# Meta rows of an output projection computed from one 34-column stationary operand

## The chip, the cores and the metric

The kernel is one program on one core of a Trainium2 chip. A core has TensorE (PE in the profile; PEld is its loading of stationary operands), VectorE (DVE), ScalarE (ACT), GpSimd (POOL) and a queue SP that issues the DMA transfers. Each engine takes its own instructions in a fixed order and waits at the first that is not ready. The metric is the device time of one execution in microseconds (us), lower is better.

## The reference

One layer of a hybrid decoder on 1024 tokens of width 1024, with 16 learned meta tokens put in front:

```python
h = concat([meta, x])                       # 1040 rows
a = rmsnorm(h, ln_mix_pre)
dq, dk, dv, hq, hf, hi, hg = split(a @ w_in)
mix = concat([diff_attention(dq, dk, dv), hgrn2(hq, hf, hi, hg)]) @ w_out
h = h + rmsnorm(mix, ln_mix_post)
a = rmsnorm(h, ln_ffn_pre)
u = causal_conv(a @ w_up, width 3)          # token t sees t-2, t-1, t
h = h + rmsnorm((gelu(gate) * up) @ w_down, ln_ffn_post)
return h[16:]
```

The meta rows are dropped at the end. After the mixing step only the last two of them still matter, because the width-3 convolution of the first real token looks back at two rows. So the output projection `@ w_out` is computed for 1024 token rows and two meta rows.

## The kernel before, in words

All large products are made in split precision: an operand is kept as a rounded part (`hi`) and a remainder (`lo`), and a product is three matmuls, hi·hi, hi·lo and lo·hi. A split of a weight tile is a copy on ACT (the rounded part) and a subtraction on POOL or DVE (the remainder); `split` is that helper. Recorded through a helper, every DVE, ACT and POOL instruction has line L54, so tiles, and not lines, tell them apart.

The stretch that matters lies between the last input projections and the feed-forward network:

- **First half of the output projection** (`out_first`): output columns 0 to 511, token blocks 1 to 8 in order, for the seven 128-row slices k = 0 to 6 of the mixed features. Each block is 21 matmuls of 512 columns (lines L972, L974, L976 in `out_part`; tile `py`, stationary operand `mp`). Behind block 4 come the two meta rows (stationary `m`, two columns wide): 7 slices × 3 matmuls. Slice k = 7 is not there yet: it is the last head of the HGRN recurrence, `hgrn_head`, which is interleaved with these matmuls by `interleave`, by a count of estimated PE time. That head has a pass over seven levels (tile `pl`, lines L417 and L423); between two levels DVE multiplies `kr` and `hq`, and the next level's matmuls read the result. Then follow the state chain (`pk`, `kn`, `pu`, `st`, `po`) and the normalised outputs (`on`, `ss`).
- Meanwhile the weights of the second half (`wor1`, split into `woh` and `wol`, `load_wo`) and those of the feed-forward network (`ra`, split into `uh` and `ul`, `prep_plain` and `prep`) are loaded and split. A raw tile can be overwritten by a later load only when its split is done, so SP waits for POOL or DVE there.
- **Second half**: columns 512 to 1023, the same blocks, all eight slices. Block 1 is followed by the meta rows (tile `py1_0`, 8 slices × 3 matmuls), then `out_last` for some blocks, which adds slice 7 to the first half (tile `pz`). `post(i)` normalises a block on ACT and DVE, adds the residual and normalises again; `trans(i)` transposes the result on PE (L1174, tile `pa`) two blocks later, `post(0)`'s during block 4.

PE's order is the order written in the program. The orders on DVE, ACT, POOL and SP in this part are chosen by a scheduler from the dependencies and its own estimates, except where `issue_after` ties an instruction to another.

Of the kernel before, what the change touches and what calls it, by code (L numbers as in the profile page):

```python
# [9 lines left out]
F32 = mybir.dt.float32  # L10
F32R = mybir.dt.float32r
U8 = mybir.dt.uint8
AF = mybir.ActivationFunctionType
ALU = mybir.AluOpType
# [3 lines left out]
P = 128  # L18
META = 16
SEQ = 1024  # L20
L = META + SEQ
D = 1024
KD = D // P
# [63 lines left out]
def layer_kernel(ctx: ExitStack, tc: tile.TileContext, x, meta, table, lbl, gpre, gpost, win,  # L87
# [3 lines left out]
    V, A = Ordered(tc, nc.vector, state), Ordered(tc, nc.scalar, state)  # L91
    G = Ordered(tc, nc.gpsimd, state)
    T, SY = nc.tensor, nc.sync
# [19 lines left out]
    def const(shape, name, dt=F32):  # L113
        return cp.tile(shape, dt, tag=name, name=name)
# [12 lines left out]
    nlam = const([P, 1], "nlam")  # L127
    cwt = const([P, 2 * NF, 3], "cwt")
    cbt = const([P, 2 * NF], "cbt")
    m0 = const([P, 2, KD, 2], "m0", F32R)  # L130

    hsc = dp.tile([SEQ, D], F32, tag="hsc", name="hsc")
    gsc = dp.tile([DFF, SEQ], F32, tag="gsc", name="gsc")
# [390 lines left out]
    def normed(k, b0, src, on, ss, C, n, gain, nm, raw=None, gate=None):  # L524
        if gate is None:
            V.scalar_tensor_tensor(ss[:C, :n], ss[:C, :n], 1.0 / 128, ss[:C, 4:4 + n], ALU.mult, ALU.add)
            A.activation(ss[:C, :n], ss[:C, :n], AF.Ln)
            A.activation(ss[:C, :n], ss[:C, :n], AF.Exp, scale=-0.5)
        else:
            rstd_of(ss[:C, :n], ss[:C, :n], 128.0)  # L530
        V.tensor_tensor(on[:C, :n], src, ss[:C, :n].rearrange("p (n o) -> p n o", o=1).to_broadcast([C, n, P]), op=ALU.mult)
        yield 1
        pt = ps_m(f"ss{nm}")
        W = start(b0 + n - 1) + rows(b0 + n - 1) - start(b0)
        for c in range(n):
            o = max(W - (n - c) * C, 0)
            T.transpose(pt[:, o:o + C], on[:C, c], ident[:C, :C])
        if gate is None:
            raw = on.rearrange("p n c -> p (n c)")[:, :W]
            A.mul(raw, pt[:, :W], gain)  # L540
        else:
            V.scalar_tensor_tensor(raw, pt[:, :W], gain, gate, ALU.mult, ALU.mult)

        def halves(hi, lo, cols):
            A.copy(hi, raw[:, cols])
            V.tensor_tensor(lo, raw[:, cols], hi.bitcast(F32), op=ALU.subtract)

        if b0 == 0:
            halves(m0[:, 0, k], m0[:, 1, k], slice(META - 2, META))
        first = max(b0, 1)  # L550
        if b0 + n > first:
            w = P * (b0 + n - first)
            m = parts_tile(nm)
            halves(m[:, 0, :w], m[:, 1, :w], slice(W - w, W))
            parts_store(k, first, b0 + n, m, 0)
        yield 1
# [410 lines left out]
    def out_part(m, py, wo, ks, first, last):  # L967
        r = m.shape[-1]
        for k in ks:
            hi, lo = wo[k]  # L970
            mh, ml = m[:, 0, k], m[:, 1, k]
            T.matmul(py[:r], mh, hi, start=(first and k == ks[0]), stop=False)  # L972
            yield 216
            T.matmul(py[:r], mh, lo, start=False, stop=False)  # L974
            yield 216
            T.matmul(py[:r], ml, hi, start=False, stop=(last and k == ks[-1]))  # L976
            yield 216

    SLOTS = (("X1", "X2", "mp", "X1", "X2", "mp", "X1", "X2"), ("mp", "X1", "X2", "mp", "X1", "X2", "X1", "mp"))

    def block_tile(n, i):
# [30 lines left out]
    def out_last(p):  # L1012
        r = tok(p)[0]
        py = ps_b(f"pz{p}")
        m = m0[:, :, KD - 1:] if p == 0 else k7(p)
        for _ in out_part(m, py, wo0[KD - 1:], range(1), True, True):
            pass
        V.tensor_tensor(y0[:r, p], y0[:r, p], py[:r], op=ALU.add)
        junk = qp.tile([P, 512], F32, tag="junk", name=f"jz{p}", bufs=1)
        A.activation(junk[:r], y0[:r, p], AF.Square, accum_out=ssy[:r, p, 0:1])  # L1020
        A.activation(ssy[:r, p, 0:1], ssy[:r, p, 0:1], AF.Identity, bias=eps[:r], scale=1.0 / D)
        if p < 3:
            y0_gain(p)

    def out_first():
        pys = {}
        steps = [(1, 0), (2, 0), (1, 1), (2, 1), (1, 2), (2, 2)] + [(i, c) for i in range(3, NBLK) for c in range(3)]
        KS = (range(0, 2), range(2, 4), range(4, 7))
        for i, c in steps:
            if c == 0:  # L1030
                pys[i] = ps_s(f"py0_{i}")[:, 0] if i < 3 else ps_in(f"py0_{i}")
                if 2 < i + 1 < NBLK:
                    first_load(i + 1)
                elif i == NBLK - 1:
                    second_load(1)
            yield from out_part(blocks[i], pys[i], wo0, KS[c], c == 0, c == 2)
            if c == 2:
                A.copy(y0[:, i], pys.pop(i))
            if i == 4 and c == 2:
                py = ps_in("py0_0")  # L1040
                yield from out_part(m0, py, wo0, range(7), True, True)
                A.copy(y0[:2, 0], py[:2])

    interleave(out_first(), [hgrn_head(t_h, set())] + carried(), FO, 4200)
    close(h_cm, at_p_cm, p_cm)
# [81 lines left out]
    def load_xh(i):  # L1127
        r = tok(i)[0]
        if i:
            xhs[i] = qp.tile([P, D], F32, tag="xh", name=f"xh{i}")  # L1130
        else:
            xhs[i] = ep.tile([P, D], F32, tag="e0", name="xh0")
        SY.dma_start(xhs[i][:r], meta[14:16, :] if i == 0 else x[P * (i - 1): P * i, :])

    def post(i, py):
        r, t0 = tok(i)
        xh = xhs.pop(i)
        if i % 2:
            a2 = long_tile(f"a2_{i}")[:, :D]
        elif i == 0:  # L1140
            a2 = xh
        else:
            a2 = bp.tile([P, D], F32, tag="a2", name=f"a2_{i}", bufs=1)
        tmp = qp.tile([P, 512], F32, tag="tmp", name=f"tmp{i}", bufs=1)
        junk = qp.tile([P, 512], F32, tag="junk", name=f"junk{i}", bufs=1)
        s1, s2 = ssy[:r, i, 1:2], ssy[:r, i, 2:3]
        A.activation(junk[:r], py[:r], AF.Square, accum_out=s1)
        V.tensor_tensor(tmp[:r], py[:r], gpo[:r], op=ALU.mult)
        A.activation(s1, s1, AF.Ln, bias=ssy[:r, i, 0:1], scale=1.0 / D)
        A.activation(s1, s1, AF.Exp, scale=-0.5)  # L1150
        V.scalar_tensor_tensor(xh[:r, :512], y0[:r, i], s1, xh[:r, :512], ALU.mult, ALU.add)
        V.scalar_tensor_tensor(xh[:r, 512:], tmp[:r], s1, xh[:r, 512:], ALU.mult, ALU.add)
        if i:
            SY.dma_start(hsc[P * (i - 1): P * i, :], xh)
        if i:
            A.activation(a2[:r], xh[:r], AF.Square, accum_out=s2)
        else:
            s3 = ssy[:r, i, 3:4]
            for half, s_ in ((0, s2), (1, s3)):
                A.activation(py[:r], xh[:r, 512 * half:512 * half + 512], AF.Square, accum_out=s_)  # L1160
            V.tensor_tensor(s2, s2, s3, op=ALU.add)
        rstd_of(s2, s2, D)
        V.scalar_tensor_tensor(a2[:r], xh[:r], s2, gfb[:r], ALU.mult, ALU.mult)
        a2t[i] = a2
# [49 lines left out]
    def run(*args):  # L1214
        for _ in out_part(*args):
            pass

    def k7(i):
        return m7[:, i - 1:i].rearrange("p b l t -> p l b t")

    for i in range(1, NBLK):
        py = ps_b(f"py1_{i}")
        if i >= 3:
            y0_gain(i)
        if i == 1:
            load_xh(1)
            load_xh(0)
        if i + 1 < NBLK:
            second_load(i + 1)
            load_xh(i + 1)  # L1230
        run(blocks[i], py, wo, range(4), True, False)
        if i == 3:
            trans(1)
        if i == 4:
            trans(0)
        if i > 3:
            trans(i - 2)
        run(blocks[i], py, wo, range(4, 7 if i == 1 else 8), False, i > 1)
        if i == 1:
            pm = ps_b("py1_0")  # L1240
            run(m0, pm, wo, range(KD), True, True)
            for p in range(3):
                out_last(p)
            run(k7(1), py, wo[KD - 1:], range(1), False, True)
            post(1, py)
            post(0, pm)
            for p in (3, 4):
                out_last(p)
            continue
        post(i, py)  # L1250
        if i == 5:
            t_split(0, 0, quarter(0, 0), ep, "e0")
            t_split(0, 4, quarter(0, 4), ep, "e1")
        if i == 7:
            t_split(0, 7, quarter(0, 7), mxp, "X2", WN[0])
            t_split(0, 6, quarter(0, 6), mxp, "X1", WN[0])
        if i in (2, 3):
            for p in (1 + 2 * i, 2 + 2 * i):
                out_last(p)
# [382 lines left out]
```

## Time and profile before

| what | value |
|---|---|
| median of 3 runs | 1322.26 us (1322.09 to 1323.52) |
| profiled execution: its time | 1325.6 us |
| profiled execution: its span | 1323.8 us |
| mean granted TensorE clock | 0.997 |
| PE busy | 1286.8 us, 97% of the span |
| DVE / ACT / POOL busy | 930.1 / 692.5 / 455.4 us |

A row of the timeline gives the start, the duration, the engine, the line, the operation, output and inputs, the shapes, and in brackets the engine's idle time just before it and what ended that. Matmuls overlap, so the start-to-start distance, not the duration, is what one costs. A row of the waits gives the total, the number and the longest wait. A row of the windows gives busy time and number of instructions of each engine in a stretch, then the granted TensorE clock, the share of DMA busy time and the GB/s.

### The profile page before, as it was taken

To read this page: it belongs to the slowest core of one execution; us is meant where nothing else is said; L and a number is where in the kernel's file an instruction comes from. 1 tells how busy PE (TensorE), PEld (TensorE's weight loads), DVE (VectorE), ACT (ScalarE), POOL (GpSimd) and SP (SyncE) were. 2 spreads that over 40 slices of the span, in tenths; PEclk is the share of its full clock that TensorE was granted. 3 is DMA by queue.
4 is the path that set the end of the run, shared out by engine and by line. 5 is a ranking of instruction groups with operands and counts; after the bars stand their busy time and mean duration, and the time that the engine had idled before them with its cause. 6 is when DMAs were issued, how large, how long until landed. Compare 5 with 4: busy or idle time off the path is not lost.

```text
span 1323.8 us, 26191 instructions
## 1 busy us (share of the span) xinstructions
PE 1286.8 (97%) x10172; PEld 1185.5 (90%) x10172; DVE 930.1 (70%) x1531; ACT 692.5 (52%) x1635; POOL 455.4 (34%) x340
## 2 busy tenths in 40 slices
PE   8999999999999999899999999999999999999997
PEld 7899999899999988677999999999999997888875
DVE  6464646465645564547997788989989967697586
ACT  8475466547544754246754444444444435454553
POOL 5211211121112111243077667676676730010121
PEclk9999999999999999999999999999999999999999
DMA  5111121112111335487232234545445428865363
GB/s 209 61 40 33 54 57 41 49 46 65 44 42 41 88 101 169 153 277 254 81 112 80 80 95 154 177 144 173 154 144 166 144 84 275 312 205 166 88 206 120
DMA packets 99427, 165.00 MB, mean 125 GB/s; under 512 B 10035, under 2 KB 34899, under 8 KB 99302
## 3 DMA queue, kind: packets, MB, share of 16 engines
q1 hardware_dynamic: 99302, 163.32, 37.8%
q8 instruction: 80, 1.31, 0.4%
q14 instruction: 45, 0.37, 0.1%
HBM read 122.65 MB, written 40.63 MB: 123 GB/s over the span
## 4 chain that ended last, share of the span: by engine, by line
PE 45%; DVE 11%; ACT 3%; issue 3%; DMA 2%; POOL 0%; SPq 0%; DVEq 0%; ACTq 0%; POOLq 0%
PE pd L1491 5%; PE pd L1492 5%; PE pd L1490 5%; DVE c L54 5%; PE pb L1316 4%; PE pb L1317 3%; PE pb L1318 3%; PE pa L1316 2%; PE pa L1317 2%; PE pa L1318 2%; PE pc L1316 2%; PE pc L1317 2%; PE pc L1318 2%; PE py L976 1%; PE py L972 1%
## 5 line engine op out<-in xcount | busy, mean ns | idle before, releaser
L1316 PE MATMUL pb<-t,uh 128*128 128x258 f32 x504 | 144.0, 286 | 8.9 <-DVE u L54 8.9
L1318 PE MATMUL pb<-t,ul 128*128 128x258 f32 x504 | 141.6, 281 | 0.0
L1317 PE MATMUL pb<-t,uh 128*128 128x258 f32 x504 | 141.6, 281 | 0.0
L1491 PE MATMUL pd<-wl,gh 128*128 128x512 f32 x308 | 122.0, 396 | 1.2 <-DVE wl L54 1.1
L1492 PE MATMUL pd<-wh,gl 128*128 128x512 f32 x308 | 121.7, 395 | 0.0
L1490 PE MATMUL pd<-wh,gh 128*128 128x512 f32 x308 | 121.7, 395 | 0.0
L54 POOL TENSOR_TENSOR c<-c,c 128x514 f32<-128x514 f32 (+1 forms) x44 | 75.2, 1709 | 121.1 <-ACT c L54 111.4
L1316 PEld LDWEIGHTS pb<-t,uh 128*128 128x128 f32 x504 | 95.4, 189 | 12.2 <-DVE u L54 12.1
L54 DVE SCALAR_TENSOR_TENSOR c<-uu,cwt,c 128x514 f32<-128x514 f32 (+1 forms) x88 | 89.2, 1023 | 19.3 <-ACT c L54 19.0
L1317 PEld LDWEIGHTS pb<-t,uh 128*128 128x128 f32 x504 | 95.6, 190 | 0.0
L1318 PEld LDWEIGHTS pb<-t,ul 128*128 128x128 f32 x504 | 95.2, 189 | 0.0
L1316 PE MATMUL pa<-t,uh 128*128 128x258 f32 (+1 forms) x336 | 95.2, 283 | 0.0
L1318 PE MATMUL pa<-t,ul 128*128 128x258 f32 (+1 forms) x336 | 95.0, 283 | 0.0
L1317 PE MATMUL pa<-t,uh 128*128 128x258 f32 (+1 forms) x336 | 94.8, 282 | 0.0
L1316 PE MATMUL pc<-t,uh 128*128 128x258 f32 (+1 forms) x336 | 94.4, 281 | 0.0
L1317 PE MATMUL pc<-t,uh 128*128 128x258 f32 (+1 forms) x336 | 94.0, 280 | 0.0
L1318 PE MATMUL pc<-t,ul 128*128 128x258 f32 (+1 forms) x336 | 93.7, 279 | 0.0
L54 DVE SCALAR_TENSOR_TENSOR c<-ug,cwt,c 128x514 f32<-128x514 f32 (+1 forms) x88 | 89.6, 1019 | 0.9 <-ACT c L54 0.6
L54 ACT CAST uh<-ra 128x512 fp32r<-128x512 f32 x67 | 41.0, 616 | 66.4 <-PE pb L1317 48.2
L1491 PEld LDWEIGHTS pd<-wl,gh 128*128 128x128 f32 x308 | 57.7, 187 | 16.5 <-DVE wl L54 2.7
L54 POOL TENSOR_TENSOR ul<-ws,uh 128x512 fp32r<-128x512 f32 x42 | 64.7, 1541 | 20.4 <-ACT uh L54 20.4
L1492 PEld LDWEIGHTS pd<-wh,gl 128*128 128x128 f32 x308 | 57.7, 187 | 14.4 <-DVE gl L54 0.4
(373 smaller groups left out, 4161.2 us busy)
## 6 DMA issues: line engine op xcount, KB each, us to landing
ra<-in_wup_dram SPq DMA_DIRECT2D x88, 256.0 KB, 3.0
mp<-msc SPq DMA_DIRECT2D x23, 512.0 KB, 6.0
wd<-in_wdown_dram SPq DMA_DIRECT2D x44, 256.0 KB, 3.3
tsc<-wd SPq DMA_DIRECT2D x44, 256.0 KB, 3.2
wi<-tsc SPq DMA_DIRECT2D x44, 256.0 KB, 2.9
gi<-gsc SPq DMA_DIRECT2D x33, 256.0 KB, 4.1
wi<-in_wdown_dram SPq DMA_DIRECT2D x33, 256.0 KB, 5.3
gsc<-c SPq DMA_DIRECT2D x22, 257.0 KB, 2.3
```

The costliest lines, as they stand in the source:

```text
L54: ins = call(*args, **kw)
L972: T.matmul(py[:r], mh, hi, start=(first and k == ks[0]), stop=False)
L976: T.matmul(py[:r], ml, hi, start=False, stop=(last and k == ks[-1]))
L1316: T.matmul(pt, hi[:, s], th[:, k], start=(first and k == 0), stop=False, skip_group_check=True)
L1317: T.matmul(pt, hi[:, s], tl[:, k], start=False, stop=False, skip_group_check=True)
L1318: T.matmul(pt, lo[:, s], th[:, k], start=False, stop=(k == 3), skip_group_check=True)
L1490: T.matmul(py, gh[:, s], wh, start=(k == 0 and pr not in (3, 7)), stop=False, skip_group_check=True)
L1491: T.matmul(py, gh[:, s], wl, start=False, stop=False, skip_group_check=True)
L1492: T.matmul(py, gl[:, s], wh, start=False, stop=(k == NH - 1), skip_group_check=True)
```

## The change

The two meta rows of slices 0 to 6 were kept as a tile `m0[part, slice, 2]`; now they lie in one row of 46 columns, the rounded parts at columns 2k and the remainders at 32 + 2k, the rest set to zero. Slice 7 has its own tile `m0_7`. A stationary operand of 34 columns from column 2k then holds both parts of slice k, at output rows 0 to 1 and 32 to 33 (the rows between are not used), so one matmul with `hi` gives hi·hi and lo·hi, and a second with `lo` and two columns gives hi·lo. The two pairs of rows are brought together by ACT copies and an addition on GpSimd, once in each half. In the second half slice 7 is done right behind slice 0, with three matmuls as before. `post(0)` reads the sum from SBUF and not from PSUM, and stands behind `post(2)`, no longer behind `post(1)`.

```diff
-    m0 = const([P, 2, KD, 2], "m0", F32R)
+    m0 = const([P, 46], "m0", F32R)
+    G.memset(m0.bitcast(F32), 0.0)
+    m0_7 = const([P, 2, 1, 2], "m0_7", F32R)
...
-            halves(m0[:, 0, k], m0[:, 1, k], slice(META - 2, META))
+            hl = [m0_7[:, l, 0] if k == KD - 1 else m0[:, 32 * l + 2 * k:32 * l + 2 * k + 2] for l in range(2)]
+            halves(hl[0], hl[1], slice(META - 2, META))
...
+    def meta_part(py, wo, full):
+        for k in range(KD - 1):
+            hi, lo = wo[k]
+            both = [(34, hi), (2, lo)]
+            if k == KD - 2:
+                both.reverse()
+            for i, (r, w) in enumerate(both):
+                T.matmul(py[:r], m0[:, 2 * k:2 * k + r], w, start=(k == 0 and i == 0), stop=(r == 34 and k == KD - 2))
+                yield 216
+            if k == 0 and full:
+                yield from out_part(m0_7, py, wo[KD - 1:], range(1), False, False)
...
-        m = m0[:, :, KD - 1:] if p == 0 else k7(p)
+        m = m0_7 if p == 0 else k7(p)
...
-                yield from out_part(m0, py, wo0, range(7), True, True)
+                yield from meta_part(py, wo0, False)
+                part = ap_.tile([P, L], F32, tag="q0", name="part")[:2, :512]
                 A.copy(y0[:2, 0], py[:2])
+                A.copy(part, py[32:34])
+                G.tensor_tensor(y0[:2, 0], y0[:2, 0], part, op=ALU.add)
...
-            xhs[i] = ep.tile([P, D], F32, tag="e0", name="xh0")
+            both = ep.tile([P, 2 * D], F32, tag="e0", name="xh0")
+            xhs[i], xhs["sum"] = both[:, :D], both[:, D:]
...
-    def post(i, py):
+    def post(i, py, free=None):
...
-                A.activation(py[:r], xh[:r, 512 * half:512 * half + 512], AF.Square, accum_out=s_)
+                A.activation(free[:r], xh[:r, 512 * half:512 * half + 512], AF.Square, accum_out=s_)
...
-            run(m0, pm, wo, range(KD), True, True)
+            for _ in meta_part(pm, wo, True):
+                pass
             for p in range(3):
                 out_last(p)
             run(k7(1), py, wo[KD - 1:], range(1), False, True)
             post(1, py)
-            post(0, pm)
+            ysum = xhs.pop("sum")
+            for l in range(2):
+                A.copy(ysum[:2, 512 * l:512 * l + 512], pm[32 * l:32 * l + 2])
+            G.tensor_tensor(ysum[:2, :512], ysum[:2, :512], ysum[:2, 512:], op=ALU.add)
             for p in (3, 4):
                 out_last(p)
             continue
         post(i, py)
+        if i == 2:
+            post(0, ysum[:, :512], ysum[:, 512:])
```

The scheduler's orders move with it. In the built program, on POOL the subtractions of `wor1` slices 0 and 2 stand ahead of the four `ul` subtractions of `prep_plain`, which had been ahead of them; the new addition of the meta rows stands between. On SP the four `ra` loads of `prep_plain`, the load of the meta residual and the first `ra` load of `prep` stood ahead of block 3's load and now stand around block 8's, so their ACT copies `uh` fall into the recurrence's state chain. On DVE the subtraction `wol` of `wor1` slice 3 stood between the products of levels 5 and 6 and now stands between those of levels 3 and 4; that of slice 1 moves up by one level, into the place of a `ul`, and that `ul` moves into the state chain.

## The prediction

> **What bounds the kernel now.** First the page: PE is busy almost throughout, so what PE does not issue, or does not wait for, is time, unless a wait takes its place.
>
> ```profile
> span 1323.8 us, 26191 instructions
> PE 1286.8 (97%) x10172; PEld 1185.5 (90%) x10172; DVE 930.1 (70%) x1531; ACT 692.5 (52%) x1635; POOL 455.4 (34%) x340
> ```
>
> Then the windows around the projection: PE's one lean and slow place is 530 to 550, and 540 to 550 is the only ten microseconds in which the granted clock falls while work goes on.
>
> ```profile
> 530.00:540.00 10.00, 8.51 (x188) 5.61 (x188) 7.22 (x8) 0.00 (x0) 8.10 (x6) 1.00 0.61 194
> 540.00:550.00 10.00, 7.43 (x39) 4.39 (x37) 4.62 (x8) 3.18 (x7) 0.00 (x0) 0.83 0.58 203
> ```
>
> Then the timeline of PE there: levels 5, 6 and 7 of the last recurrence head (`pl`), and the meta matmuls (`m`) between them.
>
> ```profile
> 533.65 0.40 PE L972 MATMUL py<-woh,mp 128*128 128x512 f32 x1
> 534.15 0.73 PE L423 MATMUL pl<-hq,kr 128*32 128x16 f32 x64
> 538.80 0.70 PE L417 MATMUL pl<-hq,kr 128*32 128x32 f32 x32 [1.16 <-DVE hq L54]
> 539.42 0.39 PE L972 MATMUL py<-woh,m 128*2 128x512 f32 x1
> 544.70 1.72 PE L417 MATMUL pl<-hq,kr 128*64 128x64 f32 x16 [2.57 <-DVE hq L54]
> 546.35 0.58 PE L976 MATMUL py<-woh,m 128*2 128x512 f32 x1
> 548.01 0.57 PE L972 MATMUL py<-woh,mp 128*128 128x512 f32 x1
> 548.89 0.39 PE L972 MATMUL py<-woh,mp 128*128 128x512 f32 x1
> ```
>
> Last the chain of waits, which says what held DVE back: three `ul` subtractions and a `wol` on POOL, behind them a load, its ACT copy, DVE, and only then PE.
>
> ```profile
> 530.01 5.12 POOL ul L54 x3
> 535.13 1.27 POOL wol L54
> 536.42 5.57 DMA wor<-in_wout_dram
> 542.01 0.63 ACT woh L54
> 543.27 0.69 DVE kr L54
> 543.95 0.61 DVE hq L54
> 544.70 1.72 PE pl L417 x16
> ```
>
> In DVE's timeline `wol` of `wor1` slice 3 blocks the queue for 3.81 us, and before that a product beside POOL's `ul` takes 1.79 us where it takes 0.69 without:
>
> ```profile
> 528.20 0.69 DVE L54 TENSOR_TENSOR hq<-hq,t 128x520 f32<-128x520 f32 x1
> 532.21 1.79 DVE L54 TENSOR_TENSOR hq<-hq,tt 128x520 f32<-128x520 f32 x1
> 542.66 0.69 DVE L54 TENSOR_TENSOR wol<-wor,woh 128x512 fp32r<-128x512 f32 x1 [3.81 <-ACT woh L54]
> ```
>
> **Removed matmuls.** 7 + 7 matmuls go. The 24 meta matmuls of the second half, first and last:
>
> ```profile
> 580.36 0.39 PE L972 MATMUL py<-woh,m 128*2 128x512 f32 x1
> 585.67 0.40 PE L976 MATMUL py<-woh,m 128*2 128x512 f32 x1
> L972 PEld LDWEIGHTS py<-woh,mp x119: 186/188/329, 510.2 to 638.9; 128*128 128x128 f32 x119
> ```
>
> They are 5.31/23 = 0.231 us apart, and a 34-column load cannot cost more than the 128-column one, 0.188 us, which hides under that. So 14 × 0.231 = 3.2 us, 1.6 in each half; in the first half only if PE does not then wait for DVE.
>
> **The moved subtractions, first half.** PE's work and order up to level 4 are the same. POOL's `ul` no longer stand in front: `wol` of slices 0 and 2 start when the recurrence's products end.
>
> ```profile
> 528.30 6.83 POOL L54 TENSOR_TENSOR ul<-ra,uh 128x512 fp32r<-128x512 f32 x4
> 535.10 3.00 POOL L54 TENSOR_TENSOR wol<-wor,woh 128x512 fp32r<-128x512 f32 x2
> ```
>
> The first, at 3.00/2 = 1.5 us, ends at 529.8, and SP may issue `wor1` slice 3. Its landing took 5.57 us before, behind a 900 KB load. Now nothing is issued ahead of it for six microseconds. The eight landings around here, of `wor` and then of `ra`, were:
>
> ```profile
> DMA to landing us min/median/max: 3.6/4.2/5.6
> DMA to landing us min/median/max: 2.6/3.9/9.2
> ```
>
> I take 3.6, the fastest `wor`, since its queue is the emptiest; bounds 2.6 and 5.57. From landing to PE the chain above took 544.70 − 541.99 = 2.71 us (ACT copy, `wol`, `kr`, `hq`). But `wol` now blocks the products of level 4, so it is level 5 that waits: 529.8 + 3.6 + 2.7 = 536.1, not 534.15. That is 2.0 us later, a new PE wait of some 2.2 us (its work before ends near 533.9). From there nothing holds: level 5's products are ready about 2.4 us after its start (0.62 of matmuls, two products of 0.69, the handovers), and PE needs 0.62 + 11 × 0.231 = 3.2 us to get to level 6; level 7 likewise. From level 5's start to the end of level 7, 14 meta matmuls and 3 of block 5, PE needs 3 × 0.62 + 22 × 0.231 + 0.3 = 7.2 us. Before, the same place (with seven matmuls more) is the row 548.89, 14.7 us behind 534.15. So 7.5 us go: 1.6 are the matmuls, 1.16 + 2.57 the two waits, and most of the rest is the slow clock behind the second wait (level 7 takes 1.65 us from start to next matmul, the four meta matmuls 1.66 instead of 0.92). Less the 2.0 of the new wait: 5.5 us gained in this half, matmuls included. I take the clock as kept at a wait of 2.2 us: it fell at 2.57 and held at
>
> ```profile
> 681.62 0.39 PE L1316 MATMUL pb<-t,uh 128*128 128x258 f32 x1 [1.42 <-DVE u L54]
> ```
>
> which lies no nearer, so the other value, a loss of 1.65 + 1.66 − 0.62 − 0.92 = 1.8 us, stays in the range. [...]
>
> **The state chain.** The four `uh` copies, `uh` of `prep` and the five `ul` now fall here, on ACT, POOL and DVE. ACT is strictly in order: `kn` waits behind the first `uh`, whose `ra` load leaves SP behind block 7's load, near 539.2 (PE ends block 4 near 538.0, and two issues of 0.6). With block 7's 900 KB ahead I put its landing at 5 to 6 us, near 545; `pk` now stands 11 matmuls behind level 7 and ends near 546.3, 4 us earlier than before, so that copy is through. The other `uh` and `ul` follow in the gaps. `uh` of `prep` waits for a load that leaves SP behind block 8's, which waits for PE to end block 5 near 548.3: issued at 549.5, landed near 555, and the `m` copy behind it, 4 us earlier than in its row, is due near 556.5. On DVE, between level 4 and level 6 POOL's `ul` cost before: 0.2 + 1.1 + 1.1 + 1.1 on four products. The chain's steps on DVE and ACT wait for others now, by 0.3 us and more:
>
> ```profile
> 557.31 0.73 DVE L54 SCALAR_TENSOR_TENSOR st<-st,tt,pu 128x128 f32<-128x128 f32 x2 [3.06 <-PE pu L480]
> 558.37 0.56 DVE L54 TENSOR_TENSOR on<-po,nss 128x384 f32<-128x384 f32 x1 [0.33 <-ACT nss L54]
> 560.50 0.19 ACT L54 CAST m<-hq 128x2 fp32r<-128x2 f32 x1 [2.16 <-DVE hq L54]
> ```
>
> I take 0.5 us; bounds 0 and 3.5. [...]
>
> **Additions and copies.** `part` and the two `ysum` copies are ACT copies of two rows, the additions POOL instructions of two rows:
>
> ```profile
> 548.25 0.58 ACT L54 COPY y<-py 2x512 f32<-2x512 f32 x1 [3.61 <-PE py L976]
> 587.51 0.63 ACT L54 ACTIVATE jz<-y 2x512 f32<-2x512 f32 x1 [3.07 <-DVE y L54]
> 588.31 3.80 POOL L54 TENSOR_TENSOR y<-y,gpo 2x512 f32<-2x512 f32 x3 [2.83 <-ACT jz L54]
> ```
>
> They fall where ACT and POOL were idle 3.61, 3.07 and 2.83 us; 3 × 0.58 and 2 × 1.27 us, on no path: 0. The memset at the start is off the first path, which waits for a load: 0. In the second half slice 7 comes 19 matmuls earlier than before, so its `wol` is due at 581.1 of the old times:
>
> ```profile
> 579.88 1.37 DVE L54 TENSOR_TENSOR wol<-wor,woh 128x512 fp32r<-128x512 f32 x1 [2.36 <-ACT woh L54]
> ```
>
> It ends at 581.25: 0.2 us lost (0 to 1).
>
> **`post(0)` moved.** It issues no DMA itself, seven ACT and five DVE steps, and these now stand behind block 2's `xh`. That frees the way of `post(1)`, `post(2)` and `post(3)`. What was late there were the transposes of blocks 3 and 4:
>
> ```profile
> 607.79 0.65 PE L1174 MATMUL pa<-ident,xh 2*128 2x2 f32 x8
> 615.58 1.09 PE L1174 MATMUL pa<-ident,a 128*128 128x128 f32 x8 [0.52 <-DVE a L54]
> 623.09 1.09 PE L1174 MATMUL pa<-ident,a 128*128 128x128 f32 x8 [0.83 <-DVE a L54]
> ```
>
> Of these 1.35 us I take half, 0.65 (bounds 0 and 1.35). The meta transposes at 607.79 keep about 1.4 us of cover by my count; if it is gone, that is what they cost.
>
> **Sum.** 5.5 (first half) − 0.5 − 0.2 + 1.6 (second half) + 0.65 = 7.05, say 7.1 us. 1325.6 − 7.1 = 1318.5 for a profiled execution; the profiled one stands 3.3 above the median, so the median goes from 1322.26 to 1315.2. Everything behind is paced by PE and moves along.
>
> **Rivals.**
> 1. *The load lands late.* 5.57 us and not 3.6 makes level 5 wait 4.2 us, and the clock falls: 5.5 − 2.0 − 1.8 = 1.7 in the first half, 3.2 in all: 1319.0. For it: that value was measured; against it: what was ahead then is gone.
> 2. [...] The 3.5 us that POOL took from four DVE products is taken from `st`, `on` and `hq` instead. All on the path: 7.1 − 3.0 = 4.1 us: 1318.2. For it: slack of 0.33 at `on`; against it: the `ul` should end near 552, before the first `on`. [...]
> 3. *The waits only move.* The 6 us of waits and slow clock come back whole at level 5, the matmuls removed in the first half lay under them, and only the second half counts: 1.6 − 0.2 = 1.4: 1320.9, no measurable change. This is also the case in which the change does not do in the first half what it says.
> 4. *Slower: ACT's order.* Each `uh` stands ahead of `kn` or `m` and waits for a load. With the slowest `ra` landing, 9.2 us, the first comes at 548.4, some 1.3 us late for `kn` and `pu`, `uh` of `prep` at 558.7, some 2.8 late; a clock fall adds 1.8. That is 5.9 of the 7.1. It decides from 7.1 us of such waits, that is with two more late copies among the `uh`; from 9.7 it is slower by over 0.2%: 1325 and up. Against it: even the slowest landing is not enough by itself.
>
> **How the numbers follow.** 0.2% is 2.6 us, about what a measurement of this kernel tells from no change. Forecast 0.57, rival 1 0.13, rival 2 0.10: faster, 0.80. Rival 3 0.11: same. Rival 4 0.09: slower. The forecast's own range: best 5.5 + 1.0 (landing 2.6) + 1.6 + 1.35 = 9.45, worst 4.1: 1312.8 to 1318.2. The range given goes to rival 3 and leaves out rival 4: 1312.8 to 1321.0.
>
> **What would show it.** Right: PE waits about 2 us for `hq` at level 5, not at 6 or 7; the clock stays at 1.00 in 540 to 550; DVE's products take 0.7 us; 34 meta matmuls in all, 0.23 apart; the transposes of blocks 3 and 4 wait less; the second half's meta matmuls start near 575 and not at 580.36. Wrong: a wait over 2.5 us at level 5 with a clock below 1; ACT idle before `uh` with `kn`, `m` or `on` behind it; DVE `st` and `on` at twice their time; PE waits at `pu`, `po`, `ss`.

## The result: slower by 0.2%

The changed kernel takes 1324.87 us (median of 14 executions, 1323.72 to 1328.93) where the kernel before takes 1322.38 (14 executions beside them, 1321.17 to 1324.17). The ratio is 1.0022, 95% interval 1.0015 to 1.0029: slower by about 2.5 us. The forecast was 1315.2 with 80% for faster.

The profiled execution of the changed kernel takes 1325.23 us, near its median. First the page, then the windows (ten microseconds each, columns as in the prediction):

```profile
span 1323.4 us, 26161 instructions
PE 1288.0 (97%) x10158; PEld 1189.8 (90%) x10158; DVE 931.0 (70%) x1531; ACT 695.3 (53%) x1638; POOL 452.6 (34%) x343
```
```profile
530.00:540.00 10.00, 8.96 (x191) 5.90 (x191) 6.16 (x13) 2.71 (x6) 0.48 (x1) 1.00 0.79 244
540.00:550.00 10.00, 10.00 (x62) 8.08 (x60) 4.36 (x9) 4.77 (x9) 5.06 (x5) 1.00 0.62 186
...
600.00:610.00 10.00, 7.36 (x35) 5.89 (x34) 7.88 (x9) 7.06 (x23) 3.71 (x3) 0.83 0.49 170
```

14 matmuls are gone (10172 to 10158), and yet PE is busy 1.2 us longer. The slow place has moved: 540 to 550 runs at full clock, and 600 to 610 is slow instead. In PE's timeline of the last head's levels, the waits at levels 6 and 7 are gone:

```profile
531.18 0.69 PE L425 MATMUL pl<-hq,kr 128*32 128x16 f32 x62 [1.04 <-DVE hq L54]
534.60 0.74 PE L425 MATMUL pl<-hq,kr 128*32 128x16 f32 x64
536.53 0.40 PE L989 MATMUL py<-woh,m 128*34 128x512 f32 x1
538.02 0.70 PE L419 MATMUL pl<-hq,kr 128*32 128x32 f32 x32
541.33 1.15 PE L419 MATMUL pl<-hq,kr 128*64 128x64 f32 x16
545.07 0.49 PE L477 MATMUL pk<-ident,kr 128*128 128x128 f32 x3
```

Level 7 starts at 541.33 and not 544.70. So what was forecast for this place came. What took it back stands in the second half, at the transposes of the meta row and behind them:

```profile
603.42 0.65 PE L1193 MATMUL pa<-ident,xh 2*128 2x2 f32 x8 [2.64 <-DVE xh L54]
604.00 1.44 PE L1193 MATMUL pa<-ident,a 128*128 128x128 f32 x8
605.09 0.78 PE L975 MATMUL py<-woh,mp 128*128 128x512 f32 x1
605.66 0.63 PE L977 MATMUL py<-wol,mp 128*128 128x512 f32 x1
606.09 0.63 PE L979 MATMUL py<-woh,mp 128*128 128x512 f32 x1
```

PE waits 2.64 us for `xh`, and then its matmuls come 0.43 apart (606.09 − 605.66) instead of 0.23.

To see where time goes I use four landmarks in PE's timeline: the last `E` matmuls of the attention heads, the first `pk` of the last recurrence head, the first `pz` and the first `pq` (start of the up projection); the fourth stretch ends at the first `pd` (down projection). Before, they start at 490.29, 549.83, 585.91, 639.79 and 1096.5; in the changed kernel at 490.14, 545.07, 578.25, 635.28 and 1096.0. Stretches in us:

| profile | E to pk | pk to pz | pz to pq | pq to pd |
|---|---|---|---|---|
| before (1325.6) | 59.5 | 36.1 | 53.9 | 456.7 |
| changed (1325.2) | 54.9 | 33.2 | 57.0 | 460.7 |

Two stretches gain 7.5 us together, and two lose 7.1: the post-normalisation 3.1 and, unforeseen, the up projection 4.0, which the change does not touch. Of these 4.0 some 1.5 are a slower pace of its matmuls (see the first half alone, below); most of the other 2.5 stands behind a wait of 1.97 us at 815.41, where the clock falls a second time (0.83 in 810 to 820). And one thing doesn't fit: the two profiled executions are 0.4 us apart, the medians 2.5 the other way.

### The profile page after: what moved, and what is told of

Its sections match the earlier page's. It is cut to its first block, busy times and chain, and to the rows that moved or that the text cites. A ratio compares the mean times of both kernels' runs of the same rounds, so it can differ in the third digit from the quotient of the medians.

```text
span 1323.4 us, 26161 instructions
## 1 busy us (share of the span) xinstructions
PE 1288.0 (97%) x10158; PEld 1189.8 (90%) x10158; DVE 931.0 (70%) x1531; ACT 695.3 (53%) x1638; POOL 452.6 (34%) x343
## 4 chain that ended last, share of the span: by engine, by line
PE 39%; DVE 10%; issue 2%; ACT 2%; DMA 1%; POOL 0%; SPq 0%; DVEq 0%; ACTq 0%; POOLq 0%
PE pd L1516 5%; PE pd L1517 5%; PE pd L1515 5%; DVE c L54 5%; PE pb L1341 3%; PE pb L1343 3%; PE pb L1342 3%; PE pa L1341 2%; PE pa L1342 2%; PE pa L1343 2%; PE pc L1341 2%; PE pc L1343 2%; PE pc L1342 2%; DVE ul L54 2%; DVE t L54 1%
```

## The experiments

Each ratio is to the kernel before, timed beside it. The theories are named in the expectations: A, the late meta row; B, the up projection gives back whatever comes early; C, the profiled execution of the kernel before was not a usual one; D, came from the first four profiles: the addresses of the tiles; E, that these addresses choose the course of the stretch before `pk`.

**Only the move undone.** post(0) goes back behind post(1):

```diff
+            post(0, ysum[:, :512], ysum[:, 512:])
             for p in (3, 4):
...
-        if i == 2:
-            post(0, ysum[:, :512], ysum[:, 512:])
```

> The changed kernel with post(0) back behind post(1), so that only the move of the meta normalisation is undone. Theory A (the meta row is late: trans(0) waits 2.64 us for xh at 603.42 of the changed kernel's profile, and the slow clock behind it costs 0.9, the rest of the kernel passes a gain on): the wait is gone, the waits of 0.5 and 0.8 us at the transposes of blocks 3 and 4 come back, 1324.9 - 3.5 + 1.3 = 1322.7. Theory B (the FFN takes back whatever comes early: PE waits there for DVE's u): the wait is gone and block 8's transposes come some 2 us earlier, but the time stays at 1324 to 1325.5. Theory C (the profiled execution of the kernel before, 3.2 us above its median, showed waits that a usual execution does not have): the time is that of A, and the gain of the first half is smaller than the 7 us seen between the two profiles.

Measured: 1322.93 us, ratio 1.0003 (0.9994 to 1.0012). The move alone costs 1.9 us (1324.87 − 1322.93). From `pz` to `pq` it takes 55.1 us: better than 57.0 but not the 53.9 of before. The up projection takes 458.5.

**The transposes one block later.**

```diff
-        if i == 4:
-            trans(0)
         if i > 3:
             trans(i - 2)
+        if i == 5:
+            trans(0)
```

> The changed kernel with trans(0), the eight transposes of the meta row, one block later (behind the first four slices of block 5 and trans(3)); post(0) stays where the change put it. Theory A: no PE wait for xh, clock 1.00 in 600 to 610, 1324.9 - 3.5 = 1321.4, so 0.1% faster than before. Theory B: PE is 8 us ahead of the kernel before at block 8's transposes and the time is still 1324 to 1325.5, with more waits at pb for u. Theory C: 1321.4 too, and 8 us less in the profile than the profile of before at block 8.

Measured: 1327.23 us, ratio 1.0034 (1.0021 to 1.0047), slower still. PE's timeline and the window of this kernel:

```profile
612.20 1.97 PE L1193 MATMUL pa<-ident,a 128*128 128x128 f32 x8 [2.82 <-DVE a L54]
```
```profile
610.00:620.00 10.00, 7.80 (x31) 6.48 (x32) 7.32 (x7) 6.54 (x18) 1.07 (x1) 0.66 0.76 235
```

The wait did not go, it went to block 3's `a`. So it is not the place of the transposes alone: the blocks behind the meta row are late on DVE too. Its timeline in the changed kernel shows with what:

```profile
594.40 0.74 DVE L54 SCALAR_TENSOR_TENSOR xh<-tmp,ssy,xh 128x512 f32<-128x512 f32 x1
595.06 1.79 DVE L54 SCALAR_TENSOR_TENSOR xh<-y,ssy,xh 2x512 f32<-2x512 f32 x1
596.78 0.67 DVE L54 TENSOR_TENSOR tmp<-xh,gpo 2x512 f32<-2x512 f32 x1
...
597.98 0.73 DVE L54 SCALAR_TENSOR_TENSOR xh<-tmp,ssy,xh 2x512 f32<-2x512 f32 x1
...
599.83 1.23 DVE L54 TENSOR_TENSOR ssy<-ssy 2x1 f32<-2x1 f32 x1
...
602.09 1.27 DVE L54 SCALAR_TENSOR_TENSOR xh<-xh,ssy,gfb 2x1024 f32<-2x1024 f32 x1 [0.42 <-ACT ssy L54]
```

Two rows cost DVE as much as 128 (0.73 against 0.74): the five steps of the meta row hold it 5.7 us. They start behind block 2's `xh`, 17 us after the meta rows' last matmul at 578.02, and end at 603.36, where PE already waits; block 3's chain queues behind them. Before the change the same five started at 593.42, 8 us after the last meta matmul (585.67), and ended at 601.59, 6 us ahead of the transposes at 607.79. They held DVE about as long (5.4 us); only their place in its queue differs. First and last of them in DVE's timeline of the kernel before:

```profile
593.42 0.73 DVE L54 SCALAR_TENSOR_TENSOR xh<-y,ssy,xh 2x512 f32<-2x512 f32 x1
...
599.88 1.71 DVE L54 SCALAR_TENSOR_TENSOR xh<-xh,ssy,gfb 2x1024 f32<-2x1024 f32 x1
```

**The kernel before, once more, as it is.**

> The kernel before, unchanged: a second profile of it, and what this measurement makes of no change. Ratio 1.000 within 0.001. Theories A and B: the waits of 1.16 and 2.57 us at levels 6 and 7 and the clock of 0.83 in 540 to 550 stand in this profile too, and the profiled time is again near 1325. Theory C: at least one of them is absent or much shorter, or the profiled time is near 1322.

Measured: 1321.92 us, ratio 0.9999 (0.9990 to 1.0008), so the measurement is even. Its profiled execution took 1324.13 and had the same waits (1.17 and 2.15 us, clock 0.83). That spoke against theory C, wrongly, as the last experiment shows.

**The first half alone.** The second half's 24 meta matmuls and post(0) as before the change:

```diff
-            for _ in meta_part(pm, wo, True):
-                pass
+            for k in range(KD):
+                mh, ml = (m0_7[:, 0, 0], m0_7[:, 1, 0]) if k == KD - 1 else (m0[:, 2 * k:2 * k + 2], m0[:, 32 + 2 * k:34 + 2 * k])
+                T.matmul(pm[:2], mh, wo[k][0], start=(k == 0), stop=False)
+                T.matmul(pm[:2], mh, wo[k][1], start=False, stop=False)
+                T.matmul(pm[:2], ml, wo[k][0], start=False, stop=(k == KD - 1))
...
+            post(0, pm, pm)
```

> The change in the first half alone: the meta rows of the first half as 34 columns, the second half's meta matmuls as the 24 of two columns, post(0) behind post(1) as before the change. Theory A: 3.9 to 4.7 us gained up to the k-state product stay (the difference at pk between the profiles), no late meta row: 1322.4 - 4 = 1318.4. Theory B: 1322 to 1324. Theory C: between 1320 and 1322.

Measured: 1322.42 us, ratio 1.0005 (0.9996 to 1.0013): no gain, though `pz` comes 5.3 us earlier than in the profile of before. From `pq` to `pd` it takes 458.2 us without a new wait. That led to theory D. PE's matmuls in the up projection were slower one by one: in every profile with the wider `m0`, and in the same amount. The first `pb` matmul of a unit comes, before and in the changed kernel, at

```profile
736.02 0.29 PE L1316 MATMUL pb<-t,uh 128*128 128x258 f32 x1
...
755.95 0.29 PE L1316 MATMUL pb<-t,uh 128*128 128x258 f32 x1
```
```profile
731.78 0.28 PE L1341 MATMUL pb<-t,uh 128*128 128x258 f32 x1
...
751.85 0.32 PE L1341 MATMUL pb<-t,uh 128*128 128x258 f32 x1
```

that is, every 19.93 and every 20.07 us, with no wait of PE in between. By the author's count of the built program `m0` and `m0_7` take 224 bytes per partition where `m0` took 128, so the tiles that are allocated behind them lie 96 bytes higher.

**96 bytes and nothing else.** The kernel before with

```diff
     m0 = const([P, 2, KD, 2], "m0", F32R)
+    const([P, 24], "pad")
```

> The kernel before with one unused constant of 96 bytes per partition behind m0, and nothing else: the order of every engine's instructions is the same, and every tile that is allocated behind it on that side of SBUF lies 96 bytes higher, as the wider m0 of the change puts it. Theory D (the place of the tiles sets the pace of the matmuls: in the profiles with the wider m0 the 12 matmuls of a pc group in the up projection take 1298.5 and 1329 ns from the first to the last start where they take 1276.5 and 1311 in both profiles of before, and the 384-column matmuls of the input projection come 175.9 ns apart instead of 174.6): the slow figures stand here, and the time is 1322.3 + 2.2 (up projection) + 1.4 (input projection) = 1325.9. Theory B (the FFN takes back what comes early): the pace and the time are those of before, 1322.3. Theory C (only the profiled executions of before were slow): 1322.3 too.

Measured: 1324.67 us, ratio 1.0014 (1.0005 to 1.0023). An unused constant makes the kernel slower by 1.9 us by the ratio (2.7 by the medians). The pace is that of the changed kernel, 754.23 − 734.16 = 20.07:

```profile
734.16 0.28 PE L1317 MATMUL pb<-t,uh 128*128 128x258 f32 x1
...
754.23 0.31 PE L1317 MATMUL pb<-t,uh 128*128 128x258 f32 x1
```

It is less than the 3.6 of the expectation; part of the slower pace goes under waits for DVE, which shrink by 1.7 us. The waits of the up projection (total, number, longest), before and here:

```profile
PE pb L1316 <- DVE u L54: 8.9, 13, 1.4
```
```profile
PE pb L1317 <- DVE u L54: 7.2, 10, 1.4
```

**Other distances.** The changed kernel and the first half alone 128 bytes higher than before, and the kernel before 64 bytes higher:

```diff
     m0_7 = const([P, 2, 1, 2], "m0_7", F32R)
+    const([P, 8], "pad")
```

> The changed kernel with one unused constant of 32 bytes behind m0_7: the order of every engine's instructions is the same, the tiles lie 128 bytes higher than in the kernel before instead of 96. Theory D, if the pace goes by the address modulo 128 or less: the pace of before (1276.5 and 1311 ns, 174.6) and 1324.9 - 3.6 = 1321.3; if by a larger modulus: another pace, and the time moves with it. Theory B: 1324.9, unchanged.

> The change in the first half alone, with the same 32 bytes of padding. Theory D: the pace of before and 1322.4 - 3.6 = 1318.8, that is 0.26% faster than before. Theory B: 1322.4. Theory C: 1322.4, since by it the waits that the first half removes aren't there in a timed execution.

> The kernel before with 64 bytes of padding behind m0: it tells by which distance the pace goes. Theory D with a modulus of 64 or less: the pace and time of before, 1322.3. With a larger one: neither the pace of before nor that of 96 bytes need hold, and the time lies between 1320 and 1327. Theories B and C: 1322.3.

Measured: 1323.79 (ratio 1.0011, 1.0001 to 1.0021), 1321.28 (0.9992, 0.9982 to 1.0002) and 1324.28 (1.0012, 1.0003 to 1.0022). None has the pace of before in the up projection. A group of twelve `pc` matmuls over 256 columns takes 1276.5 ns from first to last start before, 1298.5 with 96 bytes, 1297 with 128 and 1312 with 64 (medians of 42 groups; over 258 columns 1311, 1329, 1337.5 and 1329). So it doesn't go by the address modulo 64 or 128, and each of the four placements has its own pace. What in the chip makes it was not tried. Nor does the pace of these groups by itself give the time: the two kernels 128 bytes higher, slow groups and all, take as long as the same kernels at the old addresses below (1323.79 and 1323.78, 1321.28 and 1321.15). A price in time is measured for 96 bytes and for 64.

**The addresses of before.** The first half alone, the whole change, and the change without its move, each with six small constants put into three tiles, so that the tiles behind them have their old addresses (some weight buffers excepted, which the whole change moves already). Every engine's order stays.

```diff
-    eps = const([P, 1], "eps")
+    cols = const([P, 2], "cols")
+    eps, one = cols[:, 0:1], cols[:, 1:2]
...
+    pair = const([P, 2], "pair")
+    sub8, gn = pair[:, 0:1], pair[:, 1:2]
...
+    conv_cols = const([P, 8 * NF], "convc")
```

> The change in the first half alone, with every tile behind the constants at its address in the kernel before: six small constants are put into three tiles, which gives back the 96 bytes. The order of every engine is that of the same kernel without this. Theory D: the pace of before (pc groups 1276.5 and 1311 ns, input projection 174.6) and 1322.4 - 2.5 = 1319.9, 0.17% faster than before: what the first half's 34 columns are worth by themselves. Theory C: 1322.3, since the waits that it removes would not be there in a timed execution.

> The whole change, with every tile behind the constants at its address in the kernel before, by the same three tiles. Theory D: the pace of before and 1324.9 - 2.5 = 1322.4; the wait of 2.6 us for the meta row's xh at the transposes stays. If instead the time stays at 1324.9, the address is not what the change lost.

> Both halves changed, post(0) back behind post(1), every tile at its address in the kernel before. Theory D: 1322.9 - 2.5 = 1320.4. Against the whole change at these addresses it gives the price of the move alone (1.9 us from the two runs without the addresses), against the first half alone the worth of the second half's seven matmuls (minus 0.5 from the runs without; 1.6 forecast).

Measured: 1321.15 (ratio 0.9988, 0.9980 to 0.9997), 1323.78 (1.0012, 1.0003 to 1.0021) and 1320.45 (0.9986, 0.9977 to 0.9995). The pace of before is back (every 755.12 − 735.18 = 19.94 in the whole change):

```profile
735.18 0.29 PE L1342 MATMUL pb<-t,uh 128*128 128x258 f32 x1
...
755.12 0.29 PE L1342 MATMUL pb<-t,uh 128*128 128x258 f32 x1
```

Against the same kernels without this, the addresses give back 1.3, 1.1 and 2.5 us; the interval of each ratio is about ±1.2 us, so these and the 1.9 to 2.7 above can be one price, some 2 us. Theory B falls: with its old pace the up projection passes on what comes early (`pq` to `pd` 456.8 in the first half alone). The last of the three, both halves without the move, has the lowest median of the study, 0.14% under the kernel before by the ratio. It and the whole change differ by the move alone, 3.3 us here and 1.9 without the addresses. The clock that was granted in every timed execution tells them apart as well: its mean is 0.996 or less in 31 of 42 executions of the four kernels with the move (this one, the changed kernel, the one with later transposes and the one 128 bytes higher) and in 7 of 66 of the six that have the new meta rows without it. Profiles with no fall or one show 0.997 or 0.998, those with two falls 0.995 or 0.994. PE's waits at the transposes, first in the whole change, then without the move:

```profile
605.74 1.01 PE L1194 MATMUL pa<-ident,xh 2*128 2x2 f32 x8 [2.68 <-DVE xh L54]
```
```profile
594.03 1.09 PE L1194 MATMUL pa<-ident,a 128*128 128x128 f32 x8 [1.73 <-DVE a L54]
602.03 0.65 PE L1194 MATMUL pa<-ident,xh 2*128 2x2 f32 x8
...
616.64 1.09 PE L1194 MATMUL pa<-ident,a 128*128 128x128 f32 x8 [0.76 <-DVE a L54]
```

Even without the move, block 1's `a` is waited for 1.73 us (in the first half alone it is not waited for), so `pz` to `pq` is 55.1 where the first half alone has 54.0. That takes back 1.1 of the 1.5 that the second half's seven matmuls save (`pk` to `pz`, 34.7 to 33.2). In time the second half is worth 0.7 us (1321.15 − 1320.45), and −0.5 at the other addresses: not told from nothing.

**Seven matmuls back.** The first half alone, at the old addresses, with one matmul of two zero columns per slice:

```diff
             for i, (r, w) in enumerate(both):
+                if r == 2:
+                    T.matmul(py[:2], m0[:, 16:18], w, start=False, stop=False)
```

> The first half alone at the addresses of before, with seven matmuls of two zero columns added to the meta rows, so that it again has 21 matmuls, each engine's order else the same. If PE is what the first half waits for, it costs 7 x 0.231 = 1.6 us: 1319.9 + 1.6 = 1321.5. If they go under a wait for DVE at levels 6 and 7 or at the state products: 1319.9.

Measured: 1322.00 us, ratio 0.9993 (0.9984 to 1.0002), 0.85 more than without them. The expectation was 1.6 or 0, and the time alone doesn't decide between them. In the profile the stretch from `E` to `pk` grows from 55.0 to 57.3. From level 5 to `pk` PE takes 12.06 us with them and 10.61 without, 1.45 more, and waits for nothing in between (level 5 and `pk`, with them, then without):

```profile
535.39 0.73 PE L426 MATMUL pl<-hq,kr 128*32 128x16 f32 x64 [1.40 <-DVE hq L54]
...
547.45 0.49 PE L478 MATMUL pk<-ident,kr 128*128 128x128 f32 x3
```
```profile
535.07 0.74 PE L426 MATMUL pl<-hq,kr 128*32 128x16 f32 x64
...
545.68 0.49 PE L478 MATMUL pk<-ident,kr 128*128 128x128 f32 x3
```

So in these two profiles the matmuls are on PE's path. The whole change at the old addresses took 57.1 for the stretch too, but there the clock fell in it, behind a wait of 1.60 us:

```profile
530.00:540.00 10.00, 8.40 (x153) 5.84 (x152) 3.67 (x8) 1.25 (x4) 1.67 (x2) 0.83 0.62 201
```

**Three more profiles of the kernel before.** What remained was that the first half gains 4.6 us from `E` to `pk` between the profiles and about 1 in time.

> The kernel before, unchanged, profiled a third time. Between the last E matmul and the first pk of the last recurrence head its two profiles (1325.6 and 1324.1 us, above the median of 1322.3) take 59.5 and 59.2 us, with waits of 1.2 and 2.2 to 2.6 us at levels 6 and 7 and a clock of 0.83 behind the second; the same order 96 or 64 bytes higher took 57.7 and 56.8, with waits of 1.0 and 1.6 us at levels 4 and 5 and no fall of the clock. Theory C (the profile on which the forecast rests was one of two courses of this stretch, the longer one): at least one of three further profiles near 1322 us takes the shorter course, 57 to 58 us. Theory E (the addresses alone choose the course): all three take 59 us or more, with the clock at 0.83 in 540 to 550.

> The same, a fourth profile. Theory C: 57 to 58 us for the stretch in at least one of the three. Theory E: 59 us or more in all.

> The same, a fifth profile. Theory C: 57 to 58 us for the stretch in at least one of the three. Theory E: 59 us or more in all.

Measured: 1321.34, 1321.23 and 1321.96 us, and 56.6, 56.7 and 57.8 us from `E` to `pk`, against 59.5 and 59.2. Theory C holds and E falls. The third profile has PE waiting at levels 4 and 5, and the clock stays (PE's timeline, then the window):

```profile
530.72 0.71 PE L423 MATMUL pl<-hq,kr 128*32 128x16 f32 x63 [1.04 <-DVE hq L54]
...
535.83 0.72 PE L423 MATMUL pl<-hq,kr 128*32 128x16 f32 x64 [1.22 <-DVE hq L54]
```
```profile
540.00:550.00 10.00, 10.00 (x61) 6.88 (x60) 4.84 (x10) 3.02 (x8) 0.00 (x0) 1.00 0.48 147
```

There `wol` of slice 3 waits 1.59 us on DVE and not 3.81:

```profile
539.78 0.69 DVE L54 TENSOR_TENSOR wol<-wor,woh 128x512 fp32r<-128x512 f32 x1 [1.59 <-ACT woh L54]
```

So the kernel before has two courses of this stretch, some 2.7 us apart, and three of the five profiled executions, those with times like the median, are on the shorter or between. The forecast was made on the longest. Against the shorter course the first half alone (55.0) gains 1.6 us in this stretch, about what its seven matmuls are worth; with them back (57.3) nothing is left of the gain. By one profile each, the moved subtractions gain nothing against it.

The profiles and the time don't agree altogether: from `E` to `pz` the first half alone is 3.0 us shorter than the third profile of before, in time 1.1. Behind `pd` it takes 0.5 more, 227.5 against 227.0, and before `E` 1.1 more, 490.7 against 489.5, within what profiles of one kernel differ by there (489.2 to 490.3 before). Neither was looked into.

## Why the prediction was wrong

**First half, 5.5 less 0.5: right for the profile that it was made on.** Of the prediction's steps these held. POOL does the two `wol` ahead of the `ul`; the load lands in time (`wol` on DVE waits 1.06 us in place of 3.81); the products for levels 5 to 7 take 0.69 us on DVE; the clock stays at 1.00; level 5 to the end of level 7 takes 7.9 us (541.33 + 1.15 − 534.60; 7.2 forecast); the meta matmuls of the second half start at 574.1 (575); a 34-column load takes 0.109 us, where one of 128 columns takes 0.188. The row on DVE:

```profile
532.37 0.69 DVE L54 TENSOR_TENSOR wol<-wor,woh 128x512 fp32r<-128x512 f32 x1 [1.06 <-ACT woh L54]
```

The new wait is at level 4 (1.04 us) and not 2.2 at level 5. "PE's work and order up to level 4 are the same" left out DVE: POOL's two `wol` now run from 527.49 on, beside the products for level 4, which had taken 0.70 and 0.69 us:

```profile
527.51 1.83 DVE L54 TENSOR_TENSOR kr<-kr,t 128x520 f32<-128x520 f32 x1 [1.02 <-POOL tt L54]
529.26 1.77 DVE L54 TENSOR_TENSOR hq<-hq,t 128x520 f32<-128x520 f32 x1
```

The collision between POOL and DVE moved up, from the products for levels 5 and 6 to those for level 4, and got shorter. From `E` to `pk` the profiles differ by 4.6, and up to `pz` by 1.4 more before the second half's matmuls count (34.6 to 34.7 from `pk` to `pz` in the first half alone, 36.1 before): 6.0 against 5.0.

**The sum: the step that failed first, and the largest miss in the first half.** "1325.6 − 7.1 = 1318.5 for a profiled execution; the profiled one stands 3.3 above the median, so the median goes from 1322.26 to 1315.2." The excess of 3.3 was seen and subtracted as if it lay elsewhere. It lay in the very waits that the step removes: 59.5 us from `E` to `pk` where the executions near the median take 56.6 to 57.8. Between 1.7 and 2.9 of the 5.5 were gained only against that execution. In time, at equal addresses, the first half is worth 1.1 us at the old ones (1322.26 − 1321.15) and 2.3 at the new (1324.67 − 1322.42); by the ratios, which are to the kernel before timed beside each, 1.6 and 1.2. That is near the 1.6 of the seven matmuls, and the 3.9 for the waits and the clock are not there.

**The parts list: a step that is missing.** "Additions and copies … 0" priced the wider `m0` by its memset alone. That it moves the tiles behind it was not looked at. The 96 bytes cost some 2 us (1.1 to 2.7 in four pairs), spread over matmuls that the change does not touch, and no rival covered it. That the place is the cause is shown; why it acts is open.

**`post(0)` moved, 0.65 gained: wrong sign.** "The meta transposes at 607.79 keep about 1.4 us of cover by my count; if it is gone, that is what they cost." In three profiles they wait 2.23, 2.64 and 2.68 us, and behind the longer two the clock falls: a loss of 1.9 and 3.3 us in the two pairs. The step credited blocks 1 to 3 with the freed queue and charged the seven ACT and five DVE steps to the meta row alone. They are 5.7 us of DVE's queue, put where DVE is what the transposes wait for, so the blocks behind them are late too (2.82 us when the transposes were moved away).

**Second half, 1.6: right on PE, not in time.** `pk` to `pz` falls by 1.5 us, and 1.1 of it comes back from `pz` to `pq`, where PE now waits for block 1's `a`: at that place it is the normalisation that PE waits for. In time it is 0.7 or −0.5 us, not told from nothing.

Together, in time and at the old addresses where there is a choice: −1.1 (first half), −0.7 (second half's matmuls), +3.3 (move), +1.1 (addresses) = +2.6. These are the steps of one chain of runs from the kernel before to the changed one, so they must add up to its difference and check nothing; each is uncertain by about 1 us.

**The rivals.** None of them was it. The load was not late (rival 1). The state chain in the tail wasn't slowed (rival 2): `st` takes 0.73 us and `on` 0.56 as before. `on` starts when POOL's `ul` are done (551.3); the first `st` run beside them and take no longer (0.73), where a product for level 4 beside POOL's `wol` took 1.83. Why `st` is not slowed was not shown. POOL's and DVE's rows:

```profile
546.16 5.10 POOL L54 TENSOR_TENSOR ul<-ra,uh 128x512 fp32r<-128x512 f32 x4 [2.92 <-ACT uh L54]
```
```profile
548.75 0.73 DVE L54 SCALAR_TENSOR_TENSOR st<-st,tt,pu 128x128 f32<-128x128 f32 x2
```

Rival 3 (the waits only move, 1.4 in all) is the nearest in amount, since the waits were worth nothing in time. Its mechanism isn't what happened: level 5 has no wait in the changed kernel, and the seven matmuls were not hidden.

ACT's order (rival 4) cost the chain 0.5 us, `kn` starting 0.55 behind the end of `pk` (545.56), after a late `uh`, where it started 0.03 behind it before:

```profile
545.47 0.62 ACT L54 CAST uh<-ra 128x512 fp32r<-128x512 f32 x1 [3.57 <-DMA ra<-in_wup_dram]
546.11 0.48 ACT L54 COPY kn<-pk 128x384 f32<-128x384 f32 x1
```

"Slower" had its 9% for ACT's loads. The move stood in the text as a gain of 0.65 with bounds of 0 and 1.35: it had no bound on the side of a loss, though the cover was counted at only 1.4 us.

## What to carry to other kernels

Before a gain is read off a wait, see in more than one profiled execution that the wait is there: one that stands 3 us above the median has them somewhere, here in the very stalls that looked worth removing. When an edit changes the size of a persistent tile, look at which tiles move, and time an unused tile of the same size alone. A step over two rows held DVE as long as one over 128 (0.73 against 0.74 us), so moving it late into a queue that others wait for delays all of them.

## What the runs showed of the hardware

- The place of tiles in SBUF changed the pace of matmuls by some 1 to 3%: medians of 1276.5 to 1312 ns for the same groups of twelve (1276.5 in both first profiles of the kernel before, 1298.5 in the first ones with the wider `m0`), though an unused constant leaves their order as it is. Three displaced placements of three had slower groups than the first; two of them, 96 and 64 bytes, also cost time (1.9 and 1.6 us by the ratios).
- The clock fell behind PE waits of 1.60, 1.9, 1.97, 2.15, 2.57, 2.64, 2.68 and 2.82 us (0.66 to 0.83 in the ten microseconds around six of them, 0.77 and 0.89 around the one of 2.68, 0.98 in the hundred around the one of 1.9) and held at 1.00 behind 1.73, 2.09 and 2.23 us, so from 1.6 to 2.2 it went both ways. The one of 1.97 us, in the up projection of the changed kernel:

```profile
815.41 0.39 PE L1341 MATMUL pb<-t,uh 128*128 128x258 f32 x1 [1.97 <-DVE u L54]
```

In the profile of the kernel before the granted clock is 0.50 from 544.97 to 548.38, behind the wait of 2.57 us that ends at 544.70; in that of the changed kernel from 604.60 to 608.01 and from 816.23 to 819.64, behind the waits that end at 603.42 and 815.41. Each of these three falls lasts 3.41 us. What decides for waits between 1.6 and 2.2 the traces don't show.
- The same program took one stretch in 56.6 to 59.5 us in five executions. At which levels DVE's products meet POOL's `ul` (some 1.8 against 0.69 us), and how long the load of slice 3 is waited for (1.59 to 3.81 us), changes from one to the next.
